# RMS norms of a decoder trunk: feature sums by 32x32 turnings and one 16-column product, roots spread by a turning

## The chip, the core and the metric

The kernel runs on one core of a Trainium2 chip. A core has a tensor engine (PE, with a separate row PEld for its weight loads), a vector engine (DVE), a scalar engine (ACT), a general-purpose engine (POOL) and a sync engine (SP, which here only issues DMAs). [...] The metric is device time in microseconds, as the median of three runs; lower is better.

## The reference

Two decoder layers over 512 tokens of 1024 features. Every part begins with an RMS norm over the features. Cut to what matters here:

```python
def rmsnorm(x, g):
    return x * rsqrt(mean(x * x, axis=-1, keepdims=True) + EPS) * g

for i in range(2):
    xn = rmsnorm(h, norm_mix[i])
    h = h + (mixer_a if i == 0 else mixer_b)(xn, ...)    # gated mixer; sliding-window attention
    h = h + conv_ffn(rmsnorm(h, norm_ffn[i]), ...)       # 1024 -> 2 x 2816 -> 1024
    h = h + (p[i] @ w_in) * sigmoid(rmsnorm(h, norm_ple[i]) @ w_gate + b_gate)
    if i == 0:
        kblk, vblk = shared_kv(h, norm_kv, w_kv)         # keys and values of layer 1
return rmsnorm(h, norm_final)
```

## The kernel before

**Layout.** The state is `h[k]`, eight tiles of 128 features (partitions) by 512 tokens. A sum over features is thus a sum over the eight tiles and over the 128 partitions. Weights and activations are split in a high and a low part, and each product is three passes of PE (`mm3`: wh·xh, wh·xl, wl·xh, L182 to L184; `mm3t` with the sides exchanged, L193 to L195). A weight unit of 128x1024 is loaded raw by SP, its high part cast by ACT (`wh`, L155), its low part subtracted by DVE (`wl`, L156), with four buffers of each.

**A norm.** Class `Norm` puts the gain into the split of `h[k]` (`split_scaled`, hi on ACT at L236, lo on DVE at L237), so that a product of un-normed data can start at once, and multiplies by the root of the mean square later. The square of each tile is taken by ACT (L265) and added up on POOL (`acc`, L270; on DVE for the first norm). `begin` sums the 128 partitions: four products, each with a 128x128 slice of `acc` as the weights and a column of 1/1024 (`mean`) as the data, so that token 128c+p comes to partition p, column c. `inv_root` adds EPS on DVE (L294) and takes the power of -1/2 on POOL (L296). `rstd` brings the roots to all partitions: `spread` makes eight 128x128 diagonal tiles on DVE (high and low parts of identity times root, L306 and L307), multiplies them with a matrix of ones on PE (two products, `sp`, L310), and ACT copies the result out of PSUM (L288). The final norm does the same for 256 tokens (`final_root`, L899; `final`).

**The norms in order.** `n0` before the gated mixer, `nf0` before the first FFN, `np0` before its gate, `n1` before attention (also for the shared keys and values), `nf1` before the second FFN, `np1` before the last gate, and the final one. In an FFN `begin` stands after the first product group `up0_0`, and `rstd` after `up0_1`:

```python
mm3(ps, parts, xs, s * P)
pss.append(ps)
if j == 0:
    rstds.append((norm.begin, norm.rstd)[s]())
```

and DVE then multiplies each group by the spread roots (`hs`, L347). Before attention the spread roots scale the keys (`kf`, L578) and queries (`qf`, L591), which are split again in high and low (`kl`, L583; `q`, L598), and the scores `sc` (L698) wait for these. The column form of the roots, `rt`, scales data that has tokens on partitions (`zv` L496, `vth`/`vtl` L632 and L633, `zt` L867).

**The last gate.** For the first 256 tokens `z` (L802) multiplies `gate0` to `gate7` by the spread roots of `np1`; the other 256 tokens are turned by PE (`ht`, L837, copied out by ACT as `hT`) and gated in the turned form (`gt` on PE, then `zt`, `st`, `hT`, `yt` on DVE, ACT and POOL).

**What sets the order.** The code is written in one order, and a scheduler puts each engine's instructions in a row by its own estimates. All products take a PSUM tile from eight buffers that go round: the ninth tile waits until the reader of the first is done. DVE's row mixes `wl` units with the steps of the norm, so an instruction that waits holds up every unit queued behind it.

## Time and profile before

| | |
|---|---|
| Median of three runs | 1160.94 us (1160.83 to 1160.94) |
| Span of the profiled execution | 1159.2 us |
| Between the span and the median | 1.7 us |
| PE busy | 1144.6 us, 99% of the span |
| DVE busy | 746.8 us, 64% |
| ACT busy | 529.1 us, 46% |
| POOL busy | 77.5 us, 7% |

A row of the profile gives an engine, a line of the kernel, the operation, what it writes and reads (buffer numbers left out), its shape and its duration in microseconds; in the view in order of time the start stands first, and a bracket tells how long the engine had been idle and who released it. The view of the chain follows the work that ended last back to the start; there a matmul is counted with the time until the next one could go. A float32 product is two passes of PE and shows as two instructions; products of split data are one.

### The profile page before, as it was taken

What the parts mean: (1) busy time and instruction counts of PE and PEld (TensorE: products, weight loads), DVE (VectorE), ACT (ScalarE), POOL (GpSimd) and SP (SyncE); (2) the same over time, 40 slices, a digit from 0 to 9 for tenths busy, and PEclk for the clock granted to TensorE, in tenths of its full rate; (3) what the DMA queues carried; (4) which work ended last, traced back from release to release, by engine and by line L of the source; (5) the groups of instructions that cost most, each with busy time, mean ns of one, the idle gap of its engine ahead of it and who ended that gap; (6) DMA issues with size and microseconds to landing.
All of it is one profiled execution on the core that took longest, in us unless ns stands there. A gap on an engine that the chain in (4) does not pass through costs nothing.

```text
span 1159.2 us, 13837 instructions
## 1 busy us (share of the span) xinstructions
PE 1144.6 (99%) x5460; PEld 960.3 (83%) x5460; DVE 746.8 (64%) x1171; ACT 529.1 (46%) x856; POOL 77.5 (7%) x85
## 2 busy tenths in 40 slices
PE   9999999999999999999999999999999999999996
PEld 6888888888888888888888888888888888888896
DVE  7356477763676367556877876677636773675666
ACT  6534344431344244544667874544413432344542
POOL 1000300000000000031200002100000000000222
PEclk9999999999999999999999999999999999999998
DMA  9322322323322323232133314232232233234302
GB/s 317 122 79 73 109 77 105 109 76 107 109 68 97 109 91 120 83 109 107 37 92 110 76 53 172 82 109 83 99 109 84 90 100 109 91 88 148 109 1 73
DMA packets 30736, 115.42 MB, mean 100 GB/s; under 512 B 3016, under 2 KB 14928, under 8 KB 21200
## 3 DMA queue, kind: packets, MB, share of 16 engines
q1 hardware_dynamic: 29552, 113.37, 29.0%
q10 hardware_dynamic: 1120, 1.18, 0.3%
q8 instruction: 43, 0.70, 0.3%
q14 instruction: 21, 0.17, 0.1%
HBM read 108.24 MB, written 2.11 MB: 95 GB/s over the span
## 4 chain that ended last, share of the span: by engine, by line
PE 94%; DVE 2%; DMA 1%; ACT 1%; issue 0%; SPq 0%; POOL 0%; POOLq 0%; ACTq 0%
PE up L182 14%; PE up L184 14%; PE up L183 14%; PE d L183 8%; PE d L182 8%; PE d L184 8%; PE gate L182 2%; PE gate L184 2%; PE gate L183 2%; PE pv L756 1%; PE o L182 1%; PE o L183 1%; PE u L183 1%; PE o L184 1%; PE u L184 1%; PE u L182 1%
## 5 line engine op out<-in xcount | busy, mean ns | idle before, releaser
L156 DVE TENSOR_TENSOR wl<-wraw,wh 128x1024 fp32r<-128x1024 f32 (+2 forms) x197 | 239.2, 1216 | 135.7 <-ACT wh L155 135.2
L155 ACT CAST wh<-wraw 128x1024 fp32r<-128x1024 f32 (+1 forms) x196 | 202.1, 1033 | 266.1 <-PE d L183 131.9
L182 PE MATMUL up<-nf00h,wh 128*128 128x512 f32 x352 | 137.2, 390 | 0.0
L182 PE MATMUL up<-nf10h,wh 128*128 128x512 f32 x352 | 137.1, 389 | 0.0
L183 PE MATMUL up<-nf00l,wh 128*128 128x512 f32 x352 | 137.0, 389 | 0.0
L184 PE MATMUL up<-nf00h,wl 128*128 128x512 f32 x352 | 137.0, 389 | 0.0
L183 PE MATMUL up<-nf10l,wh 128*128 128x512 f32 x352 | 137.0, 389 | 0.0
L184 PE MATMUL up<-nf10h,wl 128*128 128x512 f32 x352 | 137.0, 389 | 0.0
L182 PE MATMUL d<-ah,wh 128*128 128x512 f32 x352 | 136.9, 389 | 0.0
L183 PE MATMUL d<-al,wh 128*128 128x512 f32 x352 | 136.9, 389 | 0.0
L184 PE MATMUL d<-ah,wl 128*128 128x512 f32 x352 | 136.9, 389 | 0.0
L351 ACT ACTIVATE c<-hs,vec 128x512 f32<-128x512 f32 x88 | 71.5, 815 | 71.7 <-DVE hs L347 71.1
L352 DVE SCALAR_TENSOR_TENSOR c<-hs,vec,c 128x511 f32<-128x511 f32 x88 | 65.8, 749 | 34.5 <-ACT c L351 34.5
L327 DVE TENSOR_TENSOR h<-h,d 128x512 f32<-128x512 f32 x56 | 38.4, 686 | 74.4 <-PE d L184 74.4
L182 PEld LDWEIGHTS up<-nf00h,wh 128*128 128x128 f32 x352 | 66.1, 188 | 13.8
L183 PEld LDWEIGHTS up<-nf10l,wh 128*128 128x128 f32 x352 | 66.1, 188 | 13.8
L184 PEld LDWEIGHTS up<-nf10h,wl 128*128 128x128 f32 x352 | 66.1, 188 | 13.8
L182 PEld LDWEIGHTS d<-ah,wh 128*128 128x128 f32 x352 | 66.1, 188 | 13.8
L183 PEld LDWEIGHTS d<-al,wh 128*128 128x128 f32 x352 | 66.1, 188 | 13.7
L184 PEld LDWEIGHTS up<-nf00h,wl 128*128 128x128 f32 x352 | 66.1, 188 | 13.7
L240 ACT CAST ah<-a 128x512 fp32r<-128x512 f32 x44 | 27.4, 622 | 109.7 <-DVE a L357 109.6
L184 PEld LDWEIGHTS d<-ah,wl 128*128 128x128 f32 x352 | 66.1, 188 | 13.6
(335 smaller groups left out, 2087.8 us busy)
## 6 DMA issues: line engine op xcount, KB each, us to landing
wraw<-in_w_up SPq DMA_DIRECT2D x44, 1024.0 KB, 4.8
wraw<-in_w_down SPq DMA_DIRECT2D x16, 896.0 KB, 4.6
wraw<-in_w_down SPq DMA_DIRECT2D x8, 1024.0 KB, 4.9
wraw<-in_w_u SPq DMA_DIRECT2D x4, 1024.0 KB, 5.8
wraw<-in_w_out SPq DMA_DIRECT2D x4, 1024.0 KB, 4.8
wraw<-in_w_gate SPq DMA_DIRECT2D x4, 1024.0 KB, 4.7
wraw<-in_w_q SPq DMA_DIRECT2D x4, 1024.0 KB, 4.9
wraw<-in_w_o SPq DMA_DIRECT2D x4, 1024.0 KB, 5.4
```

Of the source, the lines that this page charges most:

```text
L155: nc.scalar.copy(wh[:, :n], src)
L156: nc.vector.tensor_sub(wl[:, :n], src, wh[:, :n].bitcast(F32))
L182: nc.tensor.matmul(ps, wh[:, a:b], xh, start=st, stop=False)
L183: nc.tensor.matmul(ps, wh[:, a:b], xl, start=False, stop=False)
L184: nc.tensor.matmul(ps, wl[:, a:b], xh, start=False, stop=en)
L240: nc.scalar.copy(hi, src)
L327: nc.vector.tensor_add(h[m], h[m], ps)
L351: nc.scalar.activation(c, hs, AF.Identity, bias=v("conv_b", l * 2 * NJ + col), scale=cw[2])
L352: nc.vector.scalar_tensor_tensor(c[:, 1:], hs[:, : S - 1], cw[1], c[:, 1:], op0=ALU.mult, op1=ALU.add)
L756: nc.tensor.matmul(ps, lhs, rhs[:, :, e, :], start=first, stop=end)
```

## The change

The sum over partitions no longer uses the squares as weights. DVE reduces `acc` by 32x32 turnings (`fold`: a `tensor_reduce` with `apply_transpose`, 128x512 to 128x16, so that each partition holds sums over its block of 32 features for 16 of the tokens), and one product with a constant selector `sel` adds up the four blocks. The selector is made by two small DVE instructions near the start. Partition p then holds the roots of tokens 32b + (p mod 32), b = 0 to 15, and DVE's turning of the roots, each repeated 32 times, gives the 128x512 tile with every token's root on every partition. The two `sp` products, the diagonal tiles, ACT's copy and one PSUM tile of each norm are gone, and so are `ones` and `mean`. The power on POOL works on 16 columns in place of 4 (on 8 in place of 2 in the final norm). Where the column form `rt` is wanted (`n0`, `n1`, `np1`), `tokens` picks it with four POOL copies of 32x4. The last of the eight squares is added on DVE in place of POOL.

```diff
+    def selector():
+        nc.vector.tensor_reduce(lane, ident.rearrange("p (q i) -> p i q", i=SQ), axis=mybir.AxisListType.X, op=ALU.add)
+        nc.vector.tensor_scalar_mul(sel.rearrange("p (q i) -> p q i", i=SQ),
+                                    lane.unsqueeze(1).to_broadcast([P, P // SQ, SQ]), 1.0 / D)
...
-                (eng or nc.gpsimd).tensor_add(acc, self.acc, sq)
+                (eng or (nc.vector if k == KD - 1 else nc.gpsimd)).tensor_add(acc, self.acc, sq)
...
+        def gather(self):
+            self.folded = fold(self.acc, S, self.name)
...
         def begin(self):
             ps = psum(f"{self.name}ms")
-            for c in range(NC):
-                nc.tensor.matmul(ps[:, c : c + 1], self.acc[:, c * P : (c + 1) * P], mean, start=True, stop=True)
-            self.rt = inv_root(ps[:, :NC], self.name)
-            return self.rt
+            nc.tensor.matmul(ps[:, :LANES], sel, self.folded, start=True, stop=True)
+            self.root = inv_root(ps[:, :LANES], self.name)
+
+        def tokens(self):
+            rt = const.tile([P, NC], F32, tag="rt", bufs=2, name=f"{self.name}rt")
+            for q in range(4):
+                s = slice(SQ * q, SQ * (q + 1))
+                nc.gpsimd.tensor_copy(rt[s, :], self.root[s, :].rearrange("p (c q) -> p q c", q=4)[:, q, :])
+            return rt
 
         def rstd(self):
             r = tp.tile([P, S], F32, tag="rstd", name=f"{self.name}rstd")
-            nc.scalar.copy(r, spread(self.rt, NC, self.name))
+            nc.vector.transpose(r, self.root.unsqueeze(2).to_broadcast([P, LANES, SQ]))
             return r
+
+    def fold(acc, n, name):
+        folded = const.tile([P, n // SQ], F32, tag=f"fold{n}", bufs=2, name=f"{name}fold")
+        nc.vector.tensor_reduce(folded, acc.rearrange("p (b j) -> p b j", j=SQ), axis=mybir.AxisListType.X,
+                                op=ALU.add, apply_transpose=True)
+        return folded
...
-    def spread(r, n, name):
-        dh = tp.tile([P, n, P], F32R, tag="acc", name=f"{name}dh")
-        dl = tp.tile([P, n, P], F32R, tag="acc", name=f"{name}dl")
-        ps = psum(f"{name}sp")[:, : n * P]
...
     def final_root():
+        folded = fold(facc[0], N, "fin")
         ps = psum("fms")
-        for c in range(N // P):
-            nc.tensor.matmul(ps[:, c : c + 1], facc[0][:, c * P : (c + 1) * P], mean, start=True, stop=True)
-        return inv_root(ps[:, : N // P], "fin0")
+        nc.tensor.matmul(ps[:, : N // SQ], sel, folded, start=True, stop=True)
+        return inv_root(ps[:, : N // SQ], "fin0")
 
     def final(root):
-        r = spread(root, N // P, "fin0")
+        r = tp.tile([P, N], F32, tag="c1", name="fin0r")
+        nc.vector.transpose(r, root.unsqueeze(2).to_broadcast([P, N // SQ, SQ]))
```

The instructions also move in their rows. Three places follow; a row names the line, the operation, what is written and read, and the size of what is written.

PE at the first FFN's norm, before (`up_0` and `up_1` are the first product groups of the FFN, `nf0h`/`nf0l` the split data):

```order
L184 MATMUL up_0_1263<-nf00h_932,wl_1161 128x512
L281 MATMUL nf0ms<-mean,nf0acc_1226 128x1 x4
L182 MATMUL up_1_1297<-nf00h_918,wh_1156 128x512
...
L184 MATMUL up_1_1297<-nf00h_932,wl_1161 128x512
L310 MATMUL nf0sp<-nf0dh,ones 128x512
L310 MATMUL nf0sp<-nf0dl,ones 128x512
L182 MATMUL up_0_1366<-nf00h_918,wh_1255 128x512
```

After the change the four mean products there are one, `nf0ms<-nf0fold,sel` of 128x16 at the same place, and the two `sp` rows are gone. `n0`, `np0`, `nf1` and `n1` differ alike.

DVE from the norm before attention (`n1`) to the first scores, before (`k0`, `k1`, `q0_0`, `q0_1` are PSUM tiles of keys and queries, `pr0` starts the softmax on the scores `sc0`):

```order
L156 TENSOR_TENSOR wl108_4328<-wraw57_4325,wh108_4327 128x1024
L294 TENSOR_SCALAR n1m_4321<-n1ms_4316 128x4
...
L578 TENSOR_TENSOR kf1_4410<-k1_4251,n1rstd_4361 128x512
L591 TENSOR_SCALAR qf0_0_4420<-q0_0_4335,qscale_460,n1rstd_4361 128x512
L583 TENSOR_TENSOR kl0_4238<-kf0_4400,kh0_4236 64x512 x2
...
L591 TENSOR_SCALAR qf0_1_4428<-q0_1_4336,qscale_460,n1rstd_4361 128x512
L156 TENSOR_TENSOR wl110_4461<-wraw58_4458,wh110_4460 128x1024
L598 TENSOR_TENSOR q0_1_0_4430<-qf0_1_4428,q0_1_0_4430 64x512
L598 TENSOR_TENSOR q0_1_1_4431<-qf0_1_4428,q0_1_1_4431 64x512
L701 ISA pr0_4523,neg0_4524<-far_452,sc0_0_4525,nsink_483 128x128
...
L156 TENSOR_TENSOR wl111_4465<-wraw58_4458,wh111_4464 128x1024
```

The same stretch after the change:

```order
L309 TENSOR_REDUCE n1fold_4213<-n1acc7_4194 128x16
L242 TENSOR_SCALAR n11l7_3851<-h7_87,vec_79,n11h7_3850 128x512
L158 TENSOR_TENSOR wl108_4295<-wraw57_4292,wh108_4294 128x1024
L316 TENSOR_SCALAR n1m_4283<-n1ms_4281 128x16
L303 STREAM_TRANSPOSE n1rstd_4328<-n1rt_4285 128x512
L158 TENSOR_TENSOR wl109_4299<-wraw57_4292,wh109_4298 128x1024
...
L158 TENSOR_TENSOR wl110_4415<-wraw58_4412,wh110_4414 128x1024
L608 TENSOR_SCALAR qf0_1_4382<-q0_1_4303,qscale_464,n1rstd_4328 128x512
L158 TENSOR_TENSOR wl111_4419<-wraw58_4412,wh111_4418 128x1024
L615 TENSOR_TENSOR q0_1_0_4384<-qf0_1_4382,q0_1_0_4384 64x512
L615 TENSOR_TENSOR q0_1_1_4385<-qf0_1_4382,q0_1_1_4385 64x512
L650 TENSOR_SCALAR vtl_4391<-vv0_4422,n1rt_4287,vth_4390 128x4x64
```

The fold and the turning are in, the diagonal tiles out; `qf0_0` now stands behind the four `kl`, `wl111` and one `vtl` ahead of the first `pr0`, where before they stood behind it.

PE at the last gate's norm (`np1`), before, with the semaphore that an instruction waits for:

```order
L837 MATMUL ht0_1_8841<-ident_132,h7_87 128x128
L310 MATMUL np1sp_8850<-np1dh_8848,ones_113 128x512 [waits DVE_49]
L310 MATMUL np1sp_8850<-np1dl_8849,ones_113 128x512 [waits DVE_49]
L837 MATMUL ht1_0_8900<-ident_132,h0_80 128x128 [waits PE_49]
...
L182 MATMUL gate4_8950<-np10h0_6075,own199_ah4_8915 128x256 [waits Activation_49]
```

And after:

```order
L856 MATMUL ht0_1_8785<-ident_128,h7_87 128x128
L856 MATMUL ht1_0_8831<-ident_128,h0_80 128x128
...
L856 MATMUL ht1_1_8837<-ident_128,h4_84 128x128 [waits DVE_49]
...
L856 MATMUL ht1_1_8837<-ident_128,h7_87 128x128
L184 MATMUL gate4_8881<-np10h0_6029,own199_ah4_8846 128x256 [waits DVE_49]
```

With the `sp` tile gone the buffers go round one place earlier: `gate4` now takes the buffer of `gate0` and waits for DVE's `z0` to have read it, where before it took that of `ht0_1` and waited for ACT's copy. In the final norm seven of the eight products `y` with the roots now stand ahead of `zt0_1` in DVE's row; before, all stood behind it.

More of the change, by code (lines that the diff above doesn't have):

```diff
@@ L28 @@
 EPS = 1e-6
+SQ = 32
+LANES = S // SQ
 FAR = 1e37
@@ L216, in tile_yoco @@
     nc.vector.memset(one, 1.0)
-    ones = const.tile([P, P], F32R, name="ones")
-    nc.vector.tensor_copy(ones, one.to_broadcast([P, P]))
     nc.scalar.activation(const.tile([P, 1], F32, name="warm"), one, AF.Copy, scale=one)
@@ L226, in tile_yoco @@
         nc.tensor.matmul(ps, idle[:, :P], idle, start=True, stop=True)
-    mean = const.tile([P, 1], F32, name="mean")
-    nc.vector.memset(mean, 1.0 / D)
-    minus_half = const.tile([P, NC], F32, name="minus_half")
+    minus_half = const.tile([P, LANES], F32, name="minus_half")
     nc.vector.memset(minus_half, -0.5)
@@ L232, in tile_yoco @@
     make_identity(nc, ident)
+    sel = const.tile([P, P], F32, name="sel")
+    lane = const.tile([P, SQ], F32, name="lane")
+    def selector():
+        nc.vector.tensor_reduce(lane, ident.rearrange("p (q i) -> p i q", i=SQ), axis=mybir.AxisListType.X, op=ALU.add)
+        nc.vector.tensor_scalar_mul(sel.rearrange("p (q i) -> p q i", i=SQ),
+                                    lane.unsqueeze(1).to_broadcast([P, P // SQ, SQ]), 1.0 / D)
     def split_scaled(src, g, hi, lo):
@@ L297, in inv_root @@
         return r
-    def spread(r, n, name):
-        dh = tp.tile([P, n, P], F32R, tag="acc", name=f"{name}dh")
-        dl = tp.tile([P, n, P], F32R, tag="acc", name=f"{name}dl")
-        ps = psum(f"{name}sp")[:, : n * P]
-        for c in range(n):
-            rc = r[:, c : c + 1]
-            nc.vector.tensor_scalar_mul(dh[:, c, :], ident, rc)
-            nc.vector.scalar_tensor_tensor(dl[:, c, :], ident, rc, dh[:, c, :].bitcast(F32),
-                                           op0=ALU.mult, op1=ALU.subtract)
-        for d, st, en in ((dh, True, False), (dl, False, True)):
-            nc.tensor.matmul(ps, ones, d.rearrange("p a b -> p (a b)"), start=st, stop=en)
-        return ps
     def slope(hd):
@@ L337, in up @@
             parts = chunk(256, KD)
+            if j == 0:
+                norm.gather()
             pss, cs = [], []
@@ L422, in ple @@
             parts = chunk(256, KD)
+            if c == 0:
+                norm.gather()
             for j in range(2):
@@ L457, in tile_yoco @@
         n0.square(k, nc.vector)
+    selector()
     vps.append([])
     parts = chunk(S, KD)
+    n0.gather()
     for c in range(NC):
@@ L463, in tile_yoco @@
         if c == 0:
-            rt = n0.begin()
+            n0.begin()
+    rt = n0.tokens()
     far = const.tile([P, 2 * P], F32, name="far")
@@ L560, in tile_yoco @@
     parts = chunk(256, KD)
+    nm.gather()
     kps = [psum(f"k{j}") for j in range(2)]
@@ L566, in tile_yoco @@
         nm.split(k, 1)
-    rt = nm.begin()
+    nm.begin()
+    rt = nm.tokens()
     state["tags"] = [0, 1]
@@ L818, in tile_yoco @@
     parts = chunk(S, KD)
+    npl.gather()
     pss = [psum(f"gate{m}")[:, :N] for m in range(4)]
@@ L824, in tile_yoco @@
         if m == 0:
-            rt = npl.begin()
+            npl.begin()
+    rt = npl.tokens()
     turned_h = at.tile([P, VW], F32, tag="vtl", name="hT")
```

## Prediction

> **What bounds the kernel now.** First the page: its span, the busy shares and the chain.

> ```profile
> span 1159.2 us, 13837 instructions
> PE 1144.6 (99%) x5460; PEld 960.3 (83%) x5460; DVE 746.8 (64%) x1171; ACT 529.1 (46%) x856; POOL 77.5 (7%) x85
> PE 94%; DVE 2%; DMA 1%; ACT 1%; issue 0%; SPq 0%; POOL 0%; POOLq 0%; ACTq 0%
> ```

> PE is busy 99% and carries 94% of the chain. So a PE instruction taken away is worth its time, unless PE then waits. The view of PE's waits names the places where it does already:

> ```profile
> PE sc L698 <- DMA q<-qf: 1.3, 2, 1.0
> PE sc L698 <- DVE neg L701: 0.9, 1, 0.9
> PE sc L698 <- DVE q L598: 0.8, 1, 0.8
> ```

> All are in attention. The chain in order of time (start, length) prices what the change removes from PE:

> ```profile
> 152.42 0.79 PE nf0ms L281 x8
> 153.21 0.35 PE up L182
> 158.82 0.46 PE nf0sp L310 x2
> 1114.27 0.69 PE np1sp L310 x2
> 1132.80 0.34 PE fms L899 x4
> ```

> The four mean products are eight passes; `fms` with four takes 0.45 less, so a pass is 0.1125 us. Two passes remain: 6 x 0.1125 = 0.675 saved in each norm, 2 x 0.1125 = 0.225 in the final one. That a pass has 16 columns in place of one I count as nothing, since both are short beside the weight load; at worst it gives back the 0.35 - 0.23 = 0.12 that the next product loses already. The spread pair gives 0.46 (half of it, 0.23, in the final norm, which has half the tokens).

> **The prices of what is added.** Groups by line (count | busy, mean ns):

> ```profile
> L296 POOL TENSOR_TENSOR n1rt<-n1m,minus_half 128x4 f32<-128x4 f32 x1 | 1.0, 1017 | 3.3 <-DVE n1m L294 3.3
> L296 POOL TENSOR_TENSOR fin0rt<-fin0m,minus_half 128x2 f32<-128x2 f32 x1 | 0.7, 706 | 2.4 <-DVE fin0m L294 2.4
> L486 POOL TENSOR_SCALAR nsink<-sink 128x16 f32<-128x16 f32 x1 | 0.3, 317 | 0.9 <-DMA sink<-in_sinks 0.9
> L357 DVE TENSOR_TENSOR a<-a,c 128x512 f32<-128x512 f32 x44 | 30.5, 693 | 3.0 <-ACT a L356 1.6
> ```

> *The power.* Two columns 0.706, four 1.017: 0.395 + 0.1555n. For 16 columns that is 2.88, for 8 it is 1.64. Bounds: 1.02 if the columns come free, 4.07 if 16 cost four times four. I take the line, as both rows lie on it. *The fold and the turning* have no row. Per element they read one 128x512 tile, as `a` does: 0.69 each (0.42 for 256). Bounds: 0.16, the row of `nf0m` below, and 1.39, two passes. *A POOL copy of 32x4:* between nothing and the 0.32 of `nsink`; four make up to 1.3, off PE's path. The last square moved from POOL to DVE: 0.69. The two selector instructions lie in the start, ahead of any norm, under DVE's idle time there.

> [...]

> **Four norms with full gain: n0, nf0, np0, nf1.** Take `nf0`:

> ```profile
> 148.85 0.73 DVE L237 SCALAR_TENSOR_TENSOR nf00l<-h,vec,nf00h 128x512 fp32r<-128x512 f32 x1
> L281 PEld LDWEIGHTS nf0ms<-mean,nf0acc x8: 187/192/192, 152.0 to 152.9; 128*128 128x128 f32 x8
> 153.24 0.16 DVE L294 TENSOR_SCALAR nf0m<-nf0ms 128x4 f32<-128x4 f32 x1 [3.66 <-PE nf0ms L281]
> 156.99 1.23 DVE L156 TENSOR_TENSOR wl<-wraw,wh 128x1024 fp32r<-128x1024 f32 x1 [0.53 <-ACT wh L155]
> 160.85 1.28 DVE L347 TENSOR_TENSOR hs<-up,nf0rstd 128x512 f32<-128x512 f32 x2
> 170.20 0.23 PE up L182
> ```

> DVE ends `nf00l` at 149.58; the square and the fold then take until 150.96, and PE wants the sum at 152.0. Slack 1.0, in `np0` and `nf1` alike. After the sum DVE is blocked for the power (2.9), then turns (0.69) to about 156.6. Behind this wait stand `hs`, its two `c` steps and the next `wl` unit, which was done at 158.2 and now ends near 161; PE needs it for `up2`, at 170.20 - 1.13 = 169.1. Cover 8 us, so I cost it at nothing; without cover it would be 2.8. In `n0` the `zv` on ACT wait for the column roots: later by the power's 1.86 and the copies' 0 to 1.3, less the 0.675, so 1.2 to 2.5, and ACT's idle time takes that up before its next cast:

> ```profile
> 46.60 0.69 ACT L496 ACTIVATE zv<-v,n0rt 128x512 f32<-128x512 f32 x1 [2.49 <-PE v L195]
> ```

> Gain: 4 x (0.675 + 0.46) = 4.5.

> **n1: the gain is eaten.** Here PE waits for DVE:

> ```profile
> 568.78 1.40 DVE L237 SCALAR_TENSOR_TENSOR n11l<-h,vec,n11h 128x512 fp32r<-128x512 f32 x2
> 570.77 2.44 DVE L237 SCALAR_TENSOR_TENSOR n11l<-h,vec,n11h 128x512 fp32r<-128x512 f32 x2
> 575.04 0.16 DVE L294 TENSOR_SCALAR n1m<-n1ms 128x4 f32<-128x4 f32 x1 [0.70 <-PE n1ms L281]
> 581.74 1.29 DVE L578 TENSOR_TENSOR kf<-k,n1rstd 128x512 f32<-128x512 f32 x2 [2.33 <-ACT n1rstd L288]
> 588.57 1.22 DVE L156 TENSOR_TENSOR wl<-wraw,wh 128x1024 fp32r<-128x1024 f32 x1
> 589.81 1.41 DVE L598 TENSOR_TENSOR q<-qf,q 64x512 fp32r<-64x512 f32 x2
> 590.55 0.33 PE L698 MATMUL sc<-kh,q 128*128 128x128 f32 x1 [0.83 <-DVE q L598]
> ```

> The pair of `n11l` took 2.44 beside POOL's last square and 1.40 without: DVE loses 1.04 to POOL there. With the square on DVE it pays 0.69 for it and 0.69 for the fold, 0.34 more in all, so `wl108`, which ended at 575.04 - 0.70 = 574.34, ends at 574.7 and `n1m` goes then. The power ends at 577.8 (0.2 to start), the turning at 578.4, `wl109` at 579.55: `kf` starts 2.2 earlier than at 581.74. Then the order takes it back. The four `kl`, paced by ACT's casts of 0.64, end at 583.5; only then `qf0_0` (584.2), ACT's cast and the first pair of `q` (586.25); `wl110` behind its cast (587.7), `qf0_1` (588.4), and `wl111`, now ahead (589.55). The second pair of `q` starts there, against 589.81, and with `vtl` (0.4) between, the first `pr0` comes at 591.25, as before. PE comes 1.13 earlier and waits that much longer. n1: 0. Bounds: with the power at 1.02 everything is 1.86 earlier, the 0.83 goes too: +2.0; with 4.07 it is -1.2.

> [...]

> **np1 and the tail: 0.9 of 1.8.**

> ```profile
> 1110.18 0.95 PE L281 MATMUL np1ms<-mean,np1acc 128*128 128x1 f32 x8
> 1115.58 0.36 PE L182 MATMUL gate<-np10h,own_ah 128*128 128x256 f32 x1
> 1115.61 0.76 DVE L802 TENSOR_TENSOR z<-gate,np1rstd 128x256 f32<-128x256 f32 x2 [1.22 <-ACT np1rstd L288]
> 1133.51 0.15 DVE L294 TENSOR_SCALAR fin0m<-fms 128x2 f32<-128x2 f32 x1
> 1145.81 0.74 DVE L867 SCALAR_TENSOR_TENSOR zt<-gt,np1rt,row_m 128x512 f32<-128x512 f32 x1
> 1151.54 0.47 DVE L867 SCALAR_TENSOR_TENSOR zt<-gt,np1rt,row_m 128x256 f32<-128x256 f32 x1
> ```

> PE sheds 0.675 + 0.69 = 1.36 and would reach `gate4` at 1114.22. But `gate4` now waits for `z0`. The mean ends at 1110.5, the power at 1113.62, the turning at 1114.35, `z0` (0.42) at 1114.8: `gate4` goes at 1114.84, a gain of 0.74 and a new wait of 0.6. In the tail PE sheds 0.225 + 0.23 more, but DVE sets the end there. `fin0m` goes at 1132.8; DVE is blocked for the power of 8 until 1134.65, turns, and has seven `y` (0.39 each) ahead of `zt0_1`. Added up along its row, `zt1_0` comes at 1144.75 (now 1145.81) and the last `zt` at 1150.6 (now 1151.54). Gain at the end: 0.9. Bounds: 1.8, all that PE sheds, with a free power; -0.7 with the power at 4.07.

> **Sum.** 4.5 + 0 + 0.9 = 5.4 off the span of 1159.2. The profiled run's span stands 1.7 below the median, which I carry over: 1160.94 - 5.4 = 1155.5, -0.5%. A difference under 0.2% (2.3 us) is no change to this measurement.

> **Rivals.**

> *The power is nearly flat* (1.02 for 16). Then the waits at `n1` and `gate4` vanish: 4.5 + 2.0 + 1.8 = 8.3, 1152.6. For it: a 16-column POOL operation (`nsink`) takes 0.32, so columns needn't be dear. Against: 0.706 and 1.017. Chance 0.17.

> *The gain is given back at the two places with no slack*: a power toward 4.07, a turning toward 1.39, POOL's copies in DVE's way, alone or together. At the power's bound 4.5 - 1.2 - 0.7 = 2.6, 1158.3; by a dearer turning alone 5.4 - 0.55 - 0.55 = 4.3, 1156.6. Chance 0.24 for 1156.3 to 1158.6.

> *The turnings are slow, and the kernel slower.* If a turning of 512 columns takes F, the fold is late from F = 1.7 on (slack 1.0) at `nf0`, `np0`, `nf1` and `n1`, and the turning costs F - 0.69 at `n1` and `np1`. The loss is 4(F - 1.7) + 2(F - 0.69), which equals the 5.4 at F = 2.26. At F = 2.8, four times the row, it is 8.6 and the time 1164.1. For it: nothing in this kernel shows a turning on DVE. Against: every DVE row of one pass lies within 0.75. Chance 0.07.

> *The saved passes don't come out as time*, since the next weight load ends no earlier: the 0.35 after `nf0ms` shows that a short product isn't free. Then only the spread counts: 4 x 0.46 + 0.4 = 2.2, 1158.7, no change. Chance 0.07.

> **How the numbers follow.** My forecast has 0.45 (1154 to 1156.3). Faster by over 0.2% means below 1158.6: forecast, flat power, and most of the given-back cases, 0.85. Same 0.08, slower 0.07. The range runs from the flat power's 1152.6 to the 1158.3 of the power's upper bound; outside lie the slow turning, the unsaved passes and the ends.

> **What would show it.** PE: the `ms` group at two passes and 0.2 us in each norm, no `sp`. DVE: `fold` and turning at 0.69, ahead of PE's need. POOL: the power at 2.9. A PE wait of about 2 in front of the scores of `n1`, and one of 0.6 at `gate4` for `z`. The forecast is wrong if the power or a turning is far from its line, if PE waits for a fold, or if a late `wl` unit shows as a wait of `up`.

## The result, and the profile after

The changed kernel took 1158.89 us (median of 9 runs, 1156.48 to 1160.36) against 1161.32 us (median of 9, 1160.83 to 1164.58) for the kernel before in the same session. The ratio is 0.9973, with a 95% interval of 0.9963 to 0.9983: 3.1 us faster, between 2.0 and 4.3. (The two medians lie 2.4 us apart, the two means, 1161.84 and 1158.70, 3.1.) The forecast was 5.4 us. The direction held; 2.3 us of the gain are missing. Applied to the 1160.94 from which the prediction starts, the ratio gives 1157.8: inside its range of 1152.6 to 1158.3, but above the 1154 to 1156.3 that it gave its own forecast.

The profiled run lasted 1159.21 us with a span of 1157.5; that of before, 1159.2. The head of the page after, with the shares of the chain of work behind it:

```profile
span 1157.5 us, 13692 instructions
PE 1139.6 (98%) x5408; PEld 956.2 (83%) x5408; DVE 744.3 (64%) x1138; ACT 524.3 (45%) x850; POOL 85.1 (7%) x92
PE 93%; DVE 2%; DMA 1%; POOL 1%; issue 1%; ACT 1%; SPq 0%; POOLq 0%; ACTq 0%
```

PE has shed 52 instructions and 5.0 us of busy time, yet the span has shed only 1.7, and PE's share fell from 99% to 98%: PE now waits more. (Its busy time also holds some 3 us that come from a lower clock, as shown below.) Its waits in attention and at the last gate (waited for: us in total, times, longest):

```profile
PE sc L715 <- DVE q L615: 2.0, 1, 2.0
PE sc L715 <- DMA q<-qf: 2.0, 2, 1.5
PE sc L715 <- DVE neg L718: 0.5, 1, 0.5
PE gate L184 <- DVE z L819: 0.5, 1, 0.5
```

The wait for `q` was 0.8 and is 2.0, and the one for `z` is new. To show where the time went, the table takes the start of the same product in both traces and subtracts. Negative means that the changed kernel is ahead:

| place on PE | ahead, us | what happened since the row above |
|---|---|---|
| after n0, nf0, np0 | -1.25, -2.47, -3.68 | about 1.2 gained in each norm |
| after n1's mean and (absent) spread | -4.89 | 1.21 gained |
| after the first scores of `n1` | -3.32 | 1.57 given back by waits |
| 3 us later | -1.84 | 1.48 given back, no wait in it |
| second layer's attention, before and after a stretch at 672 | -2.22, -0.65 | 1.57 given back, no wait in it |
| after nf1 | -2.09 | 1.21 gained in the norm, 0.23 by shorter waits ahead of it |
| np1's mean and spread, then `gate4` | -3.48, -2.77 | 1.39 gained, 0.71 given back |
| last gate products | -3.25 | 0.48 gained in the final norm |
| last instruction | -1.68 | 1.57 given back in the tail, off PE |

Between the rows at 589 and 672 the two traces also differ by their waits in attention: before had 0.9 for `neg` in one place, after has 0.5 in another, and one wait for the queries' DMA is 1.5 instead of 1.0. Three places carry the missing time. Two of them are stretches without any wait. The view by windows names the cause (us, then busy time and count of PE, PEld, DVE, ACT and POOL, granted TensorE clock, DMA share, GB/s):

```profile
586.00:588.00 2.00, 0.97 (x6) 0.76 (x6) 1.91 (x5) 1.96 (x3) 0.00 (x0) 1.00 0.39 70
588.00:590.00 2.00, 1.66 (x11) 1.63 (x12) 1.40 (x10) 1.32 (x8) 0.00 (x0) 0.84 1.04 438
590.00:592.00 2.00, 2.00 (x11) 2.00 (x11) 0.82 (x4) 0.57 (x4) 0.00 (x0) 0.50 0.05 21
...
672.00:674.00 2.00, 2.00 (x6) 1.51 (x6) 0.83 (x4) 0.87 (x4) 0.00 (x0) 0.50 0.00 0
```

PE's row of the first scores, with its wait in the bracket:

```profile
586.84 0.33 PE L715 MATMUL sc<-kh,q 128*128 128x128 f32 x1 [2.05 <-DVE q L615]
```

The figure to read is the granted clock, the third from the end: PE is busy for the whole of 590 to 592, but at a clock of 0.50, and so in 672 to 674. Just ahead of the first of them PE had stood still for 2.05 us. In the trace's clock records the half clock lasts 3.41 us each time, so by estimate it costs up to 1.7 us of full-speed work where PE is busy throughout; the table has 1.48 and 1.57. In the kernel before, the clock record is at 1.00 from 5.4 to 1152.2 us, and PE's last product is done at 1150.2.

### The profile page after: what moved, and what is told of

It reads as the page before. It is cut to its first block, busy times and chain, and to the rows that moved or that the text cites. A ratio compares the mean times of both kernels' runs of the same rounds, so it can differ in the third digit from the quotient of the medians.

```text
span 1157.5 us, 13692 instructions
## 1 busy us (share of the span) xinstructions
PE 1139.6 (98%) x5408; PEld 956.2 (83%) x5408; DVE 744.3 (64%) x1138; ACT 524.3 (45%) x850; POOL 85.1 (7%) x92
## 3 DMA queue, kind: packets, MB, share of 16 engines
q10 hardware_dynamic: 1120, 1.18, 0.3%
## 4 chain that ended last, share of the span: by engine, by line
PE 93%; DVE 2%; DMA 1%; POOL 1%; issue 1%; ACT 1%; SPq 0%; POOLq 0%; ACTq 0%
PE up L186 14%; PE up L185 14%; PE up L184 14%; PE d L186 8%; PE d L185 8%; PE d L184 8%; PE gate L184 2%; PE gate L186 2%; PE gate L185 2%; PE pv L773 1%; PE o L184 1%; PE o L185 1%; PE o L186 1%; PE u L185 1%; PE u L184 1%; PE u L186 1%
## 5 line engine op out<-in xcount | busy, mean ns | idle before, releaser
L184 PEld LDWEIGHTS up<-nf10h,wh 128*128 128x128 f32 x352 | 66.1, 188 | 13.8
L185 PEld LDWEIGHTS up<-nf00l,wh 128*128 128x128 f32 x352 | 66.1, 188 | 13.7
```

Of the source, the lines that this page charges most:

```text
L184: nc.tensor.matmul(ps, wh[:, a:b], xh, start=st, stop=False)
L185: nc.tensor.matmul(ps, wh[:, a:b], xl, start=False, stop=False)
```

## The experiments

Theory: the four plain norms gained what was forecast; the gain at `n1` went into a longer PE wait and, beyond it, into a half clock that the wait brought on; the gain in the tail went into the `y` products, which now read both inputs from SBUF beside a POOL instruction. Rivals: the wait itself, not the clock, is the loss at `n1`; DVE's order at `n1` was poor already before the change; the longer power is what costs; the tail is set by the length of the power and the turning, not by `y`. All edits are on the changed kernel unless another is named, and each ratio is to the kernel before on the same chip (1161.49, and 1161.40 for the second set).

### The wait kept, the idle time filled

Eight products whose result is never used run ahead of the first `vv`, where PE used to stand still.

```diff
+        for _ in range(8 if c == 0 else 0):
+            nc.tensor.matmul(ps, xq[0][0][:, :P], xq[0][0], start=True, stop=True)
```

> Eight products of 128x512 on PE (0.227 us each, 1.8 us in all) whose result is overwritten stand ahead of vv0, before the first scores; nothing else moves on any engine. Theory A (PE's wait of 2.05 us ahead of the scores of n1 is what brings the half clock after it): the wait falls to about 0.25, no slice of half clock follows between the first scores and q1, the products vv stay at 0.12 us spacing, and the span is 1.5 us shorter than that of the changed kernel (1157.5), near 1156.0; the timed runs some 1 us below its median. Theory B (the half clock has another cause, and only the wait itself costs time): the products fill the wait, the half clock stays, and the span is 1157.5, the median the same.

Measured: 1155.83 us (1155.15 to 1157.98), ratio 0.9954 (0.9941 to 0.9968), span 1153.9. The wait for `q` and two of the windows:

```profile
PE sc L717 <- DVE q L615: 0.2, 1, 0.2
```

```profile
586.00:588.00 2.00, 1.22 (x10) 0.87 (x8) 1.94 (x6) 1.69 (x2) 0.00 (x0) 1.00 0.66 152
590.00:592.00 2.00, 2.00 (x16) 1.91 (x15) 1.27 (x7) 1.10 (x5) 0.00 (x0) 1.00 0.04 12
```

The kernel has more to do on PE and is faster, by 0.0019 of the ratio or 2.2 us; the two intervals overlap at their ends, so the rows carry the point. Compare the last one with that of the changed kernel: 16 products lie between 590 and 592 where 11 did, and the clock is 1.00. The scores still can't begin before `q` is there; only PE's idleness is gone. The same products taken in both traces, this kernel is 0.4 us ahead at the first scores and 1.9 ahead 6 us later. So the half clock, not the wait, is the 1.5 us of `n1` that the forecast lacked. The stretch at 672 is at full clock here too, another 1.6 of the 3.6 us by which the spans differ.

### Half of the filling

The same edit with four products instead of eight.

```diff
-        for _ in range(8 if c == 0 else 0):
+        for _ in range(4 if c == 0 else 0):
```

> As fill_n1 with four products in place of eight: 0.9 us, so PE's wait for q is 1.15 in place of 2.05 or 0.25. Theory A (the length of the wait decides): as with the waits of 0.8 to 1.1 elsewhere no half clock follows, clock 0.996 to 0.998 in all runs, median as with eight products, 1155.8. Theory B (any wait of about 1 us can do it): the half clock is there in some of the runs, their clock 0.995 or less and their time 1.5 longer.

Measured: 1157.17 us (1155.86 to 1158.79), ratio 0.9964 (0.9952 to 0.9977).

```profile
PE sc L717 <- DVE q L615: 1.1, 1, 1.1
PE sc L717 <- DVE neg L720: 0.5, 1, 0.5
```

```profile
588.00:590.00 2.00, 1.76 (x9) 1.73 (x10) 1.33 (x9) 1.39 (x7) 0.00 (x0) 0.71 0.99 414
590.00:592.00 2.00, 2.00 (x11) 2.00 (x11) 0.82 (x4) 0.46 (x3) 0.00 (x0) 0.50 0.08 29
```

Two waits of 1.1 and 0.5, not one of 2.0, and the half clock is there all the same. That the length of a single wait decides has fallen; the last section returns to PE's idle time ahead of each half clock. The time lies between that of the changed kernel and that with eight products, and the intervals overlap with both. The runs differ in their mean clock (0.993 to 0.997), the slowest run (1158.79) having the lowest, so the half clock seems to come in some of them and not in others, or to come twice; the runs without a trace don't show it.

### DVE's order at n1

`qf0_0` goes ahead of the four `kl`, and the `wl` units 110 and 111 go behind the last piece of `q`. Nothing else moves but one of SP's DMAs (of `kh`), which goes ahead of two others (of `kl`).

```diff
+            if u in (110, 111):
+                with tc.issue_after(state["split"].ins):
+                    nc.vector.tensor_sub(wl[:, :n], src, wh[:, :n].bitcast(F32))
...
+    early, at_ = scaled(qps[0], 0, 0)
+    with tc.issue_after(at_.ins):
+        for j in range(2):
+            for e in range(2):
+                nc.vector.tensor_sub(kl[j][sides[e], e, :], kfs[j][sides[e], :], kh[j][sides[e], e, :].bitcast(F32))
...
```

> Only DVE's row between the norm before attention and the first scores moves: qf0_0 stands ahead of the four kl, and wl110 and wl111 behind the second pair of q, as in the kernel before or later; every other engine's row is the same. Theory A (the scheduler's order on DVE ate n1's gain, and the long wait brought the half clock): the second pair of q starts near 583 instead of 586.1, the wait of 2.05 for q is under 0.8, the first pr comes 2 to 2.5 us earlier, no half clock follows; span 2.4 + 1.5 = 3.9 below 1157.5, less up to 0.9 if the later wait for neg comes back: 1153.6 to 1154.6. Theory B (PE waits for the roots, so for the power of 2.9 us and the turning, whatever the order): the wait stays near 2 and the span at 1157.5.

Measured: 1153.83 us (1153.36 to 1154.97), ratio 0.9934 (0.9922 to 0.9947). DVE's row at the first query and the last, of the changed kernel and then of this one (start, length):

```profile
579.85 0.75 DVE L608 SCALAR_TENSOR_TENSOR qf<-q,qscale,n1rstd 128x512 f32<-128x512 f32 x1
...
586.11 1.40 DVE L615 TENSOR_TENSOR q<-qf,q 64x512 fp32r<-64x512 f32 x2
587.94 0.34 DVE L718 CUSTOM_DVE_ANT_0 pr<-far,sc,nsink 128x128 f32<-128x128 f32 x1
```

```profile
576.59 0.73 DVE L609 SCALAR_TENSOR_TENSOR qf<-q,qscale,n1rstd 128x512 f32<-128x512 f32 x1
...
582.98 1.40 DVE L627 TENSOR_TENSOR q<-qf,q 64x512 fp32r<-64x512 f32 x2 [0.69 <-ACT q L626]
585.56 0.34 DVE L730 CUSTOM_DVE_ANT_0 pr<-far,sc,nsink 128x128 f32<-128x128 f32 x1
```

The last pair of `q` starts 3.1 us earlier, no wait for it is left among PE's waits, and no half clock appears at either place. The gain over the change alone is 0.0039 of the ratio, 4.5 us. In the traces it is 5.4, of which 2.2 at the wait, 1.4 for the half clock behind it, and 1.6 for the one at 672. The last is not shown to be the order's doing: it is absent without this edit too, with the idle time filled, half filled, and with `y` from PSUM.

### The same order in the kernel before

```diff
+            if u in (110, 111):
+                with tc.issue_after(state["split"].ins):
...
+    early, at_ = scaled(qps[0], 0, 0)
+    with tc.issue_after(at_.ins):
...
```

> The kernel before with the same edit of DVE's order ahead of the first scores (qf0_0 ahead of the kl, both wl units behind the second pair of q). It tells how much of the gain of the kernel with order and PSUM (1153.5, 8.0 below the kernel before) belongs to the order alone. Theory A (the order is worth what PE waited there, 0.83 and some 0.3 more): 0.8 to 1.7 below the kernel before. Theory B (most of the 8 is the order's): more than 3 below.

Measured: 1161.26 us (11 runs, 1160.32 to 1161.91) against 1161.40 (15 runs); ratio 0.9996 (0.9987 to 1.0004).

```profile
PE sc L710 <- DVE neg L713: 1.7, 2, 1.1
PE sc L710 <- DMA q<-qf: 1.5, 1, 1.5
PE sc L710 <- DVE q L610: 0.4, 1, 0.4
```

No difference, where a gain of 0.8 to 1.7 seemed possible. The wait for `q` did fall from 0.8 to 0.4, but the waits for `neg` rose from 0.9 to 1.7. In this kernel the order of scores on PE and of `pr` on DVE and ACT shifted along with the edit, so it isn't the pure edit of the run before. And there was little to edit: the kernel before had `qf0_0` ahead of the `kl` and `wl111` behind the first `pr0` already, so that of the units and queries ahead of the first scores only `wl110` moved. What it shows is that this order gives the kernel before nothing, so the 4.5 us above are not a gain that lay there all along. That the poor order came in with the change is shown by the rows of DVE, before and after.

### n1 in the old form

`n1` keeps the old mean products, the old root in four columns and the diagonal spread; the other norms stay new. This kernel also has the edit of `y` described next, so it is compared with that one.

```diff
-                (eng or (nc.vector if k == KD - 1 else nc.gpsimd)).tensor_add(acc, self.acc, sq)
+                (eng or (nc.vector if k == KD - 1 and self.name != "n1" else nc.gpsimd)).tensor_add(acc, self.acc, sq)
...
+            if self.name == "n1":
+                for c in range(NC):
+                    nc.tensor.matmul(ps[:, c : c + 1], self.acc[:, c * P : (c + 1) * P], mean, start=True, stop=True)
+                self.root = inv_root(ps[:, :NC], self.name)
+                return
...
+            if self.name == "n1":
+                nc.scalar.copy(r, spread(self.root, NC, self.name))
+                return r
...
```

> The changed kernel with the norm before attention in its old form (last square on POOL, four mean products, power of 4, diagonal tiles, spread pair and ACT's copy) and the final roots in PSUM; the scheduler then gives DVE the old order there. Theory A (the turned form is worth nothing at n1 with the new order and brings the half clock): PE's wait for q is 0.8 again, no half clock follows, span near 1153.4 and median near 1155.2, 2 below the kernel with PSUM alone (1157.3). Theory B (the turned form is a gain at n1 too): 1157.3 or more.

Measured: 1154.27 us (1153.82 to 1154.81), ratio 0.9939 (0.9927 to 0.9951).

```profile
PE sc L743 <- DMA q<-qf: 1.5, 2, 1.2
PE sc L743 <- DVE q L643: 0.8, 1, 0.8
PE gate L184 <- DVE z L847: 0.5, 1, 0.5
PE sc L743 <- DVE neg L746: 0.2, 1, 0.2
```

With the new `n1` the same kernel has 0.9961 (0.9948 to 0.9973). So the change loses 0.0022, 2.5 us, at `n1` (the intervals overlap by 0.0003, so the size is rough): the old form pays 1.2 more on PE and gets it back with a wait of 0.8 instead of 2.0, and then has no half clock. My forecast for `n1` was 0.

The old form also brings the old order of DVE back, so this comparison can't tell the turned form from its order. The kernel with both edits, two sections on, can: it has the new `n1` and nearly this order (one `wl` unit stands elsewhere). There PE is 1.75 us further ahead behind the first scores than here, and the ratio is 0.9930 against 0.9939, with intervals that overlap. So the turned form is no loss at `n1`; the order that the scheduler gave it is.

### y from PSUM

The final norm's turned roots go to PSUM, as the spread roots did before the change, so that each `y` reads one input from SBUF and one from PSUM.

```diff
-        r = tp.tile([P, N], F32, tag="c1", name="fin0r")
+        r = psum("fin0r")[:, :N]
```

> The turned roots of the final norm go to a PSUM tile instead of an SBUF tile; the rest is as in the changed kernel but for one y that changes places with zt0_1. Theory A (y now reads two SBUF tiles and is blocked while POOL multiplies yt, which cost one y 1.5 instead of 0.47): the three y beside POOL's yt take 1.2 instead of 2.3, the last zt comes 1.0 earlier, span 1156.5. Theory B (the tail is set by the row of ACT and DVE behind zt1_0, not by y): end within 0.2 of 1157.5.

Measured: 1157.31 us (1155.87 to 1157.99), ratio 0.9961 (0.9948 to 0.9973); the mean clocks of its five runs are 0.995 and 0.996. The tail of the changed kernel on DVE and POOL:

```profile
1134.62 2.31 DVE L926 SCALAR_TENSOR_TENSOR y<-h,vec,fin0r 128x256 f32<-128x256 f32 x3
1134.83 1.41 POOL L902 TENSOR_TENSOR yt<-hT,row_m 128x512 f32<-128x512 f32 x1 [2.19 <-DVE hT L891]
1149.86 0.47 DVE L886 SCALAR_TENSOR_TENSOR zt<-gt,np1rt,row_m 128x256 f32<-128x256 f32 x1
```

and of this kernel:

```profile
1132.53 0.87 DVE L926 SCALAR_TENSOR_TENSOR y<-h,vec,fin0r 128x256 f32<-128x256 f32 x2
1132.75 1.29 POOL L902 TENSOR_TENSOR yt<-hT,row_m 128x512 f32<-128x512 f32 x1 [2.18 <-DVE hT L891]
1146.50 0.47 DVE L886 SCALAR_TENSOR_TENSOR zt<-gt,np1rt,row_m 128x256 f32<-128x256 f32 x1
```

Both pairs stand at the same spot, a `y` row starting 0.2 us ahead of POOL's `yt`. The view by tile has the shortest, median and longest of the eight, of the changed kernel and then of this one:

```profile
L926 DVE SCALAR_TENSOR_TENSOR y<-h,vec,fin0r x8: 469/473/1517, 1133.6 to 1138.8; 128x256 f32<-128x256 f32 x8
L926 DVE SCALAR_TENSOR_TENSOR y<-h,vec,fin0r x8: 455/473/476, 1131.6 to 1135.8; 128x256 f32<-128x256 f32 x8
```

With two SBUF inputs three `y` took 2.31, one of them 1.52 alone, which is 1.05 more than the others; from PSUM none took over 0.476. In the kernel before, with the roots in PSUM, all eight lay between 0.469 and 0.477. Against the kernel before, PE's lead at its last products is 5.33 and the end keeps 5.0 of it; in the changed kernel 3.25 became 1.68. So 1.2 to 1.3 us of the tail are the `y`: 1.05 for the long one, and the rest, as far as the rows show, for the one that now stands behind `zt0_1` and fills 0.3 us in which DVE waited for ACT. The time moved by 1.4 us by the ratios, but their intervals overlap, so the trace carries this point. The half clock at `n1` was still there in this kernel, and none at 672.

### Both edits together

The order at `n1` and `y` from PSUM, as in the two diffs above.

> Both edits together: DVE's order before attention as in n1_order, and the final roots in PSUM. If both are right the gains add: 3.0 to 3.9 and 1.0, span 1152.6 to 1153.6, 1154.5 to 1155.5 in the timed runs, some 6 us below the kernel before. If the wait for z at gate4 or DVE in the tail takes it back, 1154.5 or more.

Measured: 1153.52 us (1153.01 to 1153.81), ratio 0.9930 (0.9917 to 0.9942), 8 us faster than before and 5 faster than the change alone. All five runs have a mean clock of 0.998. Against the order alone (0.9934) the edit of `y` adds nothing that the time can tell. In the traces PE's last product comes 0.72 us later than with the order alone, by longer waits at the start and in attention, and the end still comes 0.54 earlier: the tail gains 1.26, as it did without the order.

```profile
PE sc L727 <- DMA q<-qf: 2.1, 2, 1.6
PE sc L727 <- DVE neg L730: 0.6, 1, 0.6
PE gate L188 <- DVE z L831: 0.5, 1, 0.5
```

In the order's own kernel the DMA wait was 1.8. This is the lowest median of the versions that compute every root, though the interval overlaps with those of the order alone and of the old `n1`.

### A shorter power

On top of both edits the root is taken of a quarter of the columns only; the others get a constant, so the power costs what it did in four columns (1.02 us in the trace of this kernel, and 0.71 in the final norm). Three quarters of the roots are therefore not computed.

```diff
-        nc.gpsimd.tensor_tensor(r, m, minus_half[:, :n], op=ALU.pow)
+        w = n // 4 if n in (8, 16) else n
+        nc.gpsimd.tensor_tensor(r[:, :w], m[:, :w], minus_half[:, :w], op=ALU.pow)
+        if w < n:
+            nc.vector.memset(r[:, w:], 0.05)
```

> Order and PSUM as before, and POOL takes the power of only a quarter of the columns (4 of 16, 2 of 8); the others are set to a constant beforehand, so the roots of three quarters of the tokens are not computed. It measures what the longer power still costs. Theory A (the power of 2.9 holds PE at gate4 and DVE in the tail, and at n1 no longer): the wait of 0.5 for z at gate4 goes, the last zt comes 0.5 to 1.2 earlier, span 1150.4 to 1151.1, median 1152.3 to 1153.0. Theory B (it is hidden): 1153.5 as before.

Measured: 1150.94 us (1149.89 to 1151.16), ratio 0.9910 (0.9897 to 0.9924). PE's waits in attention:

```profile
PE sc L730 <- DMA q<-qf: 1.1, 1, 1.1
PE sc L730 <- DVE neg L733: 0.5, 1, 0.5
```

The wait for `z` at `gate4` (0.5) is gone, and the DMA waits are shorter by 1.0. The kernel is 0.0020 of the ratio, 2.3 us, faster than the one with both edits (the intervals overlap by 0.0007); 0.5 to 1.2 had been expected. By the same products in both traces the span's 3.4 us are 0.74 at `gate4` and 0.93 in the tail, the two places where the power was expected to hold the kernel; 1.1 in attention, mostly those DMA waits, which move from kernel to kernel (1.0 to 2.1 in the runs above) and may owe nothing to the power; and 0.64 in the products `v` ahead of the first root, which the power can't have caused. So some 1.7 us of the longer power are left at `gate4` and in the tail, and little at `n1` (0.1).

## Why the prediction was right or wrong

**The prices held.** The groups of the changed kernel (count | busy, mean ns | idle time before):

```profile
L318 POOL TENSOR_TENSOR n1rt<-n1m,minus_half 128x16 f32<-128x16 f32 x1 | 2.9, 2911 | 7.5 <-DVE n1m L316 7.5
L318 POOL TENSOR_TENSOR fin0rt<-fin0m,minus_half 128x8 f32<-128x8 f32 x1 | 1.6, 1648 | 3.1 <-DVE fin0m L316 3.1
L309 DVE TRANSPOSE_TENSOR_REDUCE nf0fold<-nf0acc 128x16 f32<-128x512 f32 x1 | 0.7, 711 | 0.0
L303 DVE STREAM_TRANSPOSE nf0rstd<-nf0rt 128x512 f32<-128x512 f32 x1 | 0.7, 711 | 3.0 <-POOL nf0rt L318 3.0
L297 POOL COPY n1rt<-n1rt 32x4 f32<-32x4 f32 x4 | 1.7, 430 | 0.2
```

Power 2.91 and 1.65 (forecast 2.88 and 1.64), fold and turning 0.71 (0.69). So the flat power and the slow turnings, two of the rivals, are out. No run shows the 0.55 by which the rival of the given-back gain makes the turning dearer at each of two places: the turning here reads a row of repeated roots in f32 and took 0.71, near the 0.69 of the row `a`.

**Four norms with full gain: right.** The chain after `nf0`:

```profile
151.13 0.13 PE nf0ms L289 x2
151.26 0.32 PE up L184
```

0.79 became 0.13, and the next product did not get longer (0.35, now 0.32), so the rival that saved passes don't come out as time is out as well. Four norms gained 4.8 in the trace, against 4.5. DVE's fold came in time everywhere, and the delayed `hs` and `wl` stayed under their cover.

**n1, the gain is eaten: the step failed by what came after the wait.** Up to the wait it went nearly as put: the second pair of `q` started at 586.11, `pr` came at 587.94, PE waited 2.05 where "about 2" stood. Measured against the kernel before, the waits took 0.36 more than PE had saved, since DVE's chain came 0.4 later than added up. But the step priced the longer wait as a wait alone. With PE this idle, 3.4 us at half clock followed, 1.5 us more, and the bounds I gave (+2.0 to -1.2) rested on the power alone. So `n1` came to -1.8 in the trace where the sum has 0. The run with the idle time filled shows that the half clock goes when the idle time does. The order of DVE's row, which the prediction read rightly and took as given, is what made the wait: with three instructions moved the wait is gone.

POOL's copies did not get in DVE's way, as the rival of the given-back gain had it: `wl109` beside them took 1.19, where the mean of the `wl` units is 1.24. It went the other way, one of the four copies taking 1.18 us beside `wl109` and the other three 0.18, so the time was lost on POOL, off the path.

**np1 and the tail: half right.** At `gate4` the gain is 0.68 (forecast 0.74) and the wait 0.47 (0.6):

```profile
1112.81 0.39 PE L184 MATMUL gate<-np10h,own_ah 128*128 128x256 f32 x1 [0.47 <-DVE z L819]
```

The tail failed. It took `y` at the 0.39 from start to start of the kernel before, where the spread roots stood in PSUM, and missed that the change also moves this operand to SBUF. Seven `y` kept their length (0.47 each, as before); the one beside POOL's `yt` took 1.52, 1.05 more, and the tail lost 1.2 to 1.3 us in sum. (The shorter power gave 0.93 in the tail, so the power counts there too, but it had its place in the forecast.) The 1.05 is nearly the price that I had read off `n11l` beside POOL's last square (2.44 against 1.40, so 1.04), and I had not looked for it at `y`. Of the forecast's 0.9, the changed kernel has 0.68 + 0.48 - 1.57 = -0.4.

**The sum.** In the trace: 4.8 at the four norms, -0.36 and -1.5 at `n1`, -1.57 for the half clock at 672, -0.4 at `np1` and the tail, and +0.7 from the other waits, which is 1.7. The ratio has 3.1, not 1.7, since the profiled run of before (1160.94) lies 0.9 under the mean of its nine and that of the changed kernel (1159.21) 0.5 over the mean of its own. The nine of the changed kernel go from 1156.48 at a mean clock of 0.996 to 1160.36 at 0.992. A stretch of 3.4 us at half clock is 1.7 of 1157, or 0.0015 of the mean clock. But the mean clock also counts the tail behind PE's last product, which is at half clock for 8.4 us in the trace of the changed kernel and for 6.9 in that of before (0.0036 and 0.0030 of it), and by estimate for 4.6 with both edits, from the mean clock of 0.998 there. So how many stretches lie under PE's work in a run without a trace isn't shown; one to three more in the slowest than in the fastest would fit.

The time, 1157.8, falls in the stretch of the rival "the gain is given back at the two places with no slack". It was right about one of the places (`n1`), but not by its mechanisms: the power took 2.91 and the turning 0.71, both within 0.03 of the forecast, and the copies, 1.72 at `n1` against up to 1.3, were off PE's path. That the time still lies in the stated range is luck in part: the range reached up to 1158.3 for a dearer power, which didn't come. What used it up, the half clocks (3.0 us in the trace) and the long `y`, stood in no term, and neither did the 0.7 that other waits gave back.

## What to carry to other kernels

Where a change makes PE arrive earlier at a place where it waits already, the longer wait may cost more than itself: in the trace of the changed kernel a half clock of 3.41 us followed twice, where PE had been idle for 1.43 and 1.47 of the 3.41 us ahead of it, and cost 1.48 and 1.57. So look in the windows for a granted clock under 1.00. Look then at what the waiting engine does in which order: with three instructions moved the changed kernel was 4.5 us faster here. And when an operand moves from PSUM to SBUF, check which POOL instruction runs beside its reader: here one `y` took 1.52 beside POOL's `yt`, where the others took 0.47.

## What the hardware showed that was not expected

The half clock came after idle times far shorter than its own length of 3.41 us: in the trace of the changed kernel after a wait of 2.05 us at `n1`, and at 672 after a wait of 1.47. With half of the idle time filled it came after waits of 1.1 and 0.5; single DMA waits of 1.5 and 1.6 (the kernel before with the new order, and the one with both edits) did not bring it.

```profile
585.95:589.36 3.41, 1.98 (x14) 1.75 (x15) 3.05 (x11) 2.69 (x6) 0.00 (x0) 1.00 0.65 219
667.87:671.28 3.41, 1.94 (x12) 1.55 (x12) 2.40 (x11) 2.50 (x10) 0.00 (x0) 1.00 0.32 67
585.44:588.86 3.42, 1.73 (x13) 1.35 (x12) 3.06 (x9) 2.92 (x6) 0.00 (x0) 1.00 0.57 163
662.57:665.98 3.41, 2.11 (x16) 1.74 (x15) 3.12 (x15) 3.26 (x13) 0.00 (x0) 1.00 0.68 183
```

PE is idle for 1.43, 1.47, 1.69 and 1.30 us. A half clock follows the first three and not the fourth. The kernel with `y` from PSUM has one too, behind 2.57 us of idle time from 584 to 588. Ahead of the window in which PE's last product ends, no other window counted so has more than 1.15 in the changed kernel, nor more than 1.02 in the kernel before, and no half clock follows any of them. Why the half clock comes isn't shown, nor from which idle time on: in these traces it followed 1.43 of 3.41 us and not 1.30, and no run varied that alone.

The DMA wait of 1.6 in the kernel with both edits brought nothing, with 1.04 us of idle time in 664 to 666 and 0.59 in 666 to 668 and a clock of 1.00 from 664 to 674, while that of 1.47 in the changed kernel was followed by a half clock. It would fit if a border between two windows divided the wait of 1.6; that is an estimate, from the 3.413 us and the four windows above. The program around 672 is the one of before; in the profile of the changed kernel PE waited 0.44 us longer there for the DMA of the queries (1.47 against 1.03), and the second half clock followed.
